# Half pages in tags of their own, no transferred lows, a sixth raw slot and other sets of seven-product pairs in a two-layer hybrid encoder

## The chip, the cores and the metric

The kernel runs on one core of one Trainium2 chip. The metric is the device time of one execution in microseconds. Before the change it is 2624.51 us, the median of three runs (2623.55 to 2626.14).

TensorE (PE in the profile) multiplies, VectorE (DVE) and ScalarE (ACT) prepare operands and combine results, GpSimd (POOL) issues one queue of transfers and does a few small powers, SyncE (SP) issues the other queue of transfers.

## The reference

Two layers of an encoder on 256 tokens of width 4096. Each layer reads its normalised input through one projection of 11264 columns, runs grouped attention on a half of the result and bidirectional retention on the other, and returns through a second projection of 4096 columns.

```python
for l in range(DEPTH):                       # DEPTH = 2, SEQ = 256, D_MODEL = 4096
    h = rmsnorm(x, norm_w[l])
    proj = h @ w_in[l]                       # 4096 x 11264
    aq, ak, av, ag, rq, rk, rv, rg = jnp.split(proj, SPLIT_POINTS, axis=-1)
    ...
    a_out = (jax.nn.silu(ag) * gqa_attention(aq, ak, av)).astype(x.dtype)
    ...
    r = bidirectional_retention(rq, rk, rv, log_gf, log_gb).transpose(0, 2, 1, 3)
    r = rmsnorm(r, ret_norm[l]).reshape(B, S, RET_WIDTH)
    r_out = (jax.nn.silu(rg.astype(jnp.float32)) * r).astype(x.dtype)
    x = x + jnp.concatenate([a_out, r_out], axis=-1) @ w_out[l]   # 4096 x 4096
return rmsnorm(x, final_norm)
```

All of it is float32. Nearly all the arithmetic is in the two projections of each layer.

## The kernel before

**Blocks and pairs.** A projection is cut into blocks of 1024 output columns: 11 blocks for the first projection of a layer (stages 0 and 2), 4 for the second (stages 1 and 3), 30 blocks in all. A block sums over 16 pairs of 128 rows (`p` 0 to 15). For one pair, the 256 tokens, the 256 rows and the 1024 columns make a 2 x 2 by 2 x 2 product of matrices. Eleven of the sixteen pairs compute it with eight products (`EIGHT_PRODUCTS`), five with seven (`SEVEN_PRODUCTS`, a Strassen-Winograd scheme). `SEVENS` has the five for each stage. The products gather in eight PSUM banks, `M1` to `M8`; `M1`, `M5`, `M6`, `M7` belong to the seven-product pairs alone and are lent to the attention and the retention between whiles.

**High and low parts.** A float32 operand is cut into a high part in the type fp32r and the rest, the low part. One product is then three matmuls: high weight by high token part, high weight by low token part (line 1461 of the kernel before), low weight by high token part (line 1471). The high part of the weights is a cast on ACT (`whi`), the low part a subtraction on DVE (`wlo`), both recorded on line 248.

**Pages.** A *page* is a weight tile of 128 x 2 x 512. Raw pages land in `wraw` (5 slots, 512 KB each, issued by SP on line 448). An eight-product pair has two pages, A and B, with four products each. A seven-product pair has four: A, the sum page T, B and the sum page U, with 2, 2, 1 and 2 products. The sums are DVE instructions (`wsum`), one of 1024 elements for T and two of 512 for U. Page B of a seven-product pair needs the second half alone, but takes a whole tile. High and low parts lie in a ring of five tiles each (`RING = 5`, tags `whi` and `wlo`): page n+5 may be begun only when page n has had its last product. `Weights.begin` begins the pages in that order.

**Transferred lows.** Some B pages (`FARS`) are *far*: a tile pair of their own (`fhi`, `flo`), where ACT casts the high part and writes its negative into `flo`, and a transfer by POOL (line 506) then adds the raw weights to it. Those pages cost DVE nothing. There are 44 of them.

**The start.** Pairs 0 and 1 of the first block are multiplied in plain float32, without a cut (`NATIVE`); their four pages wait in the tiles `fhi`, `flo` and two of `wsum`. The token operands of the other pairs are made as their chunks of two pairs land: ACT scales by the gain and casts (`x8h`, `x7h`), DVE makes the sums of a seven-product pair (`xf`) and the low parts (`x8l`, `x7l`).

**The order of the work** is fixed when the program is built. A planner walks through the matmuls, keeps its own times for PE, DVE and ACT, and puts the remaining work (`Lane` steps: combining, rotary, softmax, retention, normalisation) between the pages where `room` says that the next page's low part is still made in time. Its constants (`STEP_V`, `LANDING`, `STORE`, `EARLY`, `NEAR` and others) are costs and distances in microseconds or products. `LANDING`, `STORE` and `FETCH` are the times after which it takes a transfer as done.

Of the kernel before, what the change touches and what calls it, by code (L numbers as in the profile page):

```python
# [33 lines left out]
BLK = 32  # L34
ALL = slice(None)
PAGES = 13
RAWS = 5

RING = 5
FAR = 1  # L40

STEP_V = 1.6
STEP_S = 0.7

V_FIXED = 0.07
S_FIXED = 0.16

MM = {512: 0.2268, 256: 0.1177}
PASS = 0.1

LANDING = 11.0
STORE = 9.0
FETCH = 13.0
FAR_LANDING = 10.0
MARGIN = 0.5

RUSH = 1.5

EARLY = 0.7

ADD_AHEAD = 2.5

NEED = {"ak": 5, "ag": 3, "rk": 4, "rg": 4}

PE_REST = 1.8

TIGHT_A = 2
TIGHT_B = 3

AT_ONCE = 5  # L70

WARM = 20

SPLITS = 2

START = 1

SEVENS = ((3, 5, 7, 9, 11), (5, 7, 9, 10, 11), (3, 5, 7, 9, 11), (5, 7, 10, 11, 12))

EVER = sorted(set(_p for _s in SEVENS for _p in _s))  # L80
EIGHTS = [_p for _p in range(NP) if _p not in EVER]
# [4 lines left out]

WHOLE = 4

HOLD = 10

NEAR = 25

LATE = 20

FARS = ((2, 12), (1, 8), (12,), (15,))


AQ, AK, AV, AG, RQ, RK, RVO, RG = 0, 2048, 2560, 3072, 5120, 6144, 7168, 9216
# [105 lines left out]
EASY = ("M7",)  # L204


BANK_REST = 1.0
APART = 0.0

TOGETHER = 4  # L210

OTHER = True

TURNS = "01"

ABREAST = True
BANKS = ("M1", "M2", "M3", "M4", "M5", "M6", "M7", "M8")


# [43 lines left out]
def hybrid_encoder(  # L263
# [47 lines left out]
    def drop(n=1):  # L311

        held[0] -= n
        own(-n)
# [85 lines left out]
    class Weights:  # L400


        def __init__(self):
            self.pages = []
            for l in range(DEPTH):
                for w, n in ((w_in, N_IN), (w_out, N_OUT2)):
                    for b in range(n):
                        stage = 2 * l + (w is w_out)
                        for g in GROUPS[stage]:
                            start = (l, b) == (0, 0) and w is w_in  # L410
                            for slot in slots_of(g, stage, start):
# [24 lines left out]
            self.order = near[:RING]  # L436
            for g in self.pages:
                self.order += g.next
# [71 lines left out]

        def begin(self, g):

            g.begun = True
            if g.far:
                self.far_parts(g, self.taken())
            elif not g.seven:
                self.parts(g, self.taken(), then=self.load)
            elif g.kind == PAGE_A:
                self.sums_low(PAGE_T)
                self.a, self.b = self.taken(), self.taken()  # L520
                self.v = t(wp, [P, 2, NB], "wsum", 2)
                ve.tensor_sub(self.v, self.a, self.b[:, 0:1, :].to_broadcast([P, 2, NB]))
                self.parts(g, self.a)
            elif g.kind == PAGE_T:
                self.sums_low(PAGE_U)
                self.u = t(wp, [P, 2, NB], "wsum", 2)
                ve.tensor_add(self.u[:, 0, :], self.a[:, 1, :], self.v[:, 0, :])
                ve.tensor_sub(self.u[:, 1, :], self.u[:, 0, :], self.b[:, 1, :])
                self.load()
                self.parts(g, self.v)  # L530
            elif g.kind == PAGE_B:
                self.parts(g, self.b, (1,), self.load)
            else:
                self.parts(g, self.u)

        def sums_low(self, kind):

# [192 lines left out]
    class Turn:  # L730
# [18 lines left out]

        def step(self, forced=False):  # L750
            c = self.fetched
            if c < self.last and c < self.cut + 2 and (self.first or stored.get(c, 1e9) < now.t + (1e9 if forced else 0.0)) and held[0] + pledged() < PAGES - (2 if tasks else 0):
# [12 lines left out]
            return False  # L765
# [6 lines left out]
    using = []  # L772

    spare, taken, window, want, users, last_block = {}, {}, [0, False, 99], [0], set(), [False]

    def take_bank():

# [13 lines left out]

    def near(late=0):

        return window[1] and window[2] >= late or window[0] <= NEAR and not window[1]

    class Lane:
        def __init__(self, steps, heavy=True, need=0, own=0, owner=None, gate=None):
# [55 lines left out]
    def advance():  # L853

        clear()
        if not lanes + running():
            if waiting:
                split_step()
                return
            if turning and turning[0].step(True):  # L860
                return
        one = min(lanes + (running() or [tasks[0]]), key=lambda v: v.ready)
        now.wait(one.ready)
        one.step()
        clear()
# [464 lines left out]
    def block(after_pair, phase, then, first_order=False, order=LAST_ORDER, last=None, hurried=False):  # L1330
# [76 lines left out]
        def end_product(n, name, p, index, k, h):  # L1407
# [17 lines left out]
            if not g.uses and g in using:  # L1425
                using.remove(g)
                if g.whole:
                    for _ in range(1 if g is not weights.wholes[-1] else RING):
                        begun()
                for one in g.next:  # L1430
                    weights.begin(one)
# [401 lines left out]
```

## Time and profile before

| | |
|---|---|
| time, median of 3 runs | 2624.51 us |
| profiled execution: its own time, span of its instructions | 2624.09 us, 2622.3 us |
| DVE busy | 2231.7 us (85%), 2666 instructions |
| ACT busy | 1684.6 us (64%), 2411 instructions |
| POOL busy | 274.6 us (10%), 413 instructions |
| moved | 633.58 MB, 242 GB/s |
| granted clock of TensorE | 0.998 |

Matmuls overlap in this profile: one of 512 columns is listed with 389 ns, but the next starts 227 ns after it. A lost quarter of a microsecond can therefore hide in "busy". The weight loads (PEld) show it better: each matmul has one, of 188 ns, and in the steady state 39 ns of idle time stand ahead of it. Whatever the view of waits lists for PEld over that is time lost by TensorE.

### The profile page before, as it was taken

What the parts mean: (1) busy time and instruction counts of PE and PEld (TensorE: products, weight loads), DVE (VectorE), ACT (ScalarE), POOL (GpSimd) and SP (SyncE); (2) the same over time, 40 slices, a digit from 0 to 9 for tenths busy, and PEclk for the clock granted to TensorE, in tenths of its full rate; (3) what the DMA queues carried; (4) which work ended last, traced back from release to release, by engine and by line L of the source; (5) the groups of instructions that cost most, each with busy time, mean ns of one, the idle gap of its engine ahead of it and who ended that gap; (6) DMA issues with size and microseconds to landing.
All of it is one profiled execution on the core that took longest, in us unless ns stands there. A gap on an engine that the chain in (4) does not pass through costs nothing.

```text
span 2622.3 us, 33965 instructions
## 1 busy us (share of the span) xinstructions
PE 2604.2 (99%) x11650; PEld 2151.5 (82%) x11650; DVE 2231.7 (85%) x2666; ACT 1684.6 (64%) x2411; POOL 274.6 (10%) x413
## 2 busy tenths in 40 slices
PE   9999999999999999999999999999999999999998
PEld 7888888888888888888888888888888888878886
DVE  8798988898878889777998889898997798897768
ACT  7776667656555778556785666676565566775545
POOL 0010221120001000111101101211100010000000
PEclk9999999999999999999999999999999999999999
DMA  7888887877667766777767777778766666656775
GB/s 287 291 263 261 266 266 240 295 241 235 211 217 235 232 227 214 259 261 255 276 219 230 257 237 265 255 239 276 249 225 209 217 227 217 227 201 220 240 235 188
DMA packets 187151, 633.58 MB, mean 242 GB/s; under 512 B 22624, under 2 KB 29280, under 8 KB 186976
## 3 DMA queue, kind: packets, MB, share of 16 engines
q1 hardware_dynamic: 147760, 521.27, 56.6%
q0 software_dynamic: 39216, 110.12, 15.9%
q8 instruction: 91, 1.49, 0.2%
q14 instruction: 84, 0.69, 0.1%
HBM read 587.27 MB, written 44.04 MB: 241 GB/s over the span
## 4 chain that ended last, share of the span: by engine, by line
PE 94%; DVE 3%; issue 1%; ACT 1%; DMA 1%; SPq 0%; DVEq 0%; POOLq 0%; POOL 0%; ACTq 0%
PE M L1461 60%; PE M L1471 30%; DVE wlo L248 1%; PE M L945 1%; PE M L944 1%; PE M L943 1%; DMA wraw<-in_w_in 1%; DVE wsum L248 1%; PE M L1455 0%; ACT whi L248 0%; ACT ca L248 0%; DMA flo<-in_w_in 0%; DVE ca L248 0%; DVE x7l L248 0%; DVE ls L248 0%
## 5 line engine op out<-in xcount | busy, mean ns | idle before, releaser
L248 ACT CAST whi<-wraw 128x1024 fp32r<-128x1024 f32 (+1 forms) x912 | 878.5, 978 | 529.8 <-PE M L1461 346.2
L248 DVE TENSOR_TENSOR wlo<-wraw,whi 128x1024 fp32r<-128x1024 f32 (+1 forms) x912 | 1007.5, 1127 | 156.3 <-ACT whi L248 147.6
L1461 PE MATMUL M<-whi,x8h 128*128 128x512 f32 x2042 | 795.7, 390 | 0.2 <-DVE cb L248 0.2
L1461 PE MATMUL M<-whi,x8l 128*128 128x512 f32 x2042 | 795.2, 389 | 0.0
L1471 PE MATMUL M<-wlo,x8h 128*128 128x512 f32 x2042 | 586.3, 389 | 0.0
L1461 PE MATMUL M<-whi,x7h 128*128 128x512 f32 x1442 | 561.2, 389 | 1.0 <-ACT whi L248 1.0
L1461 PE MATMUL M<-whi,x7l 128*128 128x512 f32 x1442 | 561.0, 389 | 0.0
L248 ACT CAST whi<-wsum 128x1024 fp32r<-128x1024 f32 x300 | 315.9, 1053 | 212.4 <-PE M L1461 105.2
L1461 PEld LDWEIGHTS M<-whi,x8h 128*128 128x128 f32 x2042 | 383.4, 188 | 80.8 <-DVE cb L248 1.3
L1461 PEld LDWEIGHTS M<-whi,x8l 128*128 128x128 f32 x2042 | 383.4, 188 | 79.0 <-DVE x7l L248 0.2
L1471 PEld LDWEIGHTS M<-wlo,x8h 128*128 128x128 f32 x2042 | 382.1, 188 | 78.8
L1471 PE MATMUL M<-wlo,x7h 128*128 128x512 f32 x1442 | 442.1, 390 | 2.7 <-DVE wlo L248 2.4
L248 DVE TENSOR_TENSOR wlo<-wsum,whi 128x1024 fp32r<-128x1024 f32 x300 | 365.9, 1220 | 42.6 <-ACT whi L248 42.4
L1471 PEld LDWEIGHTS M<-wlo,x7h 128*128 128x128 f32 x1442 | 269.5, 188 | 63.3 <-DVE wlo L248 8.2
L1461 PEld LDWEIGHTS M<-whi,x7h 128*128 128x128 f32 x1442 | 270.7, 188 | 57.8 <-ACT whi L248 1.4
L1461 PEld LDWEIGHTS M<-whi,x7l 128*128 128x128 f32 x1442 | 270.7, 188 | 56.3
L248 DVE TENSOR_TENSOR wsum<-wraw 128x1024 f32<-128x1024 f32 x150 | 182.5, 1216 | 29.9 <-DMA wraw<-in_w_out 14.0
L506 POOL DMA_DIRECT2D flo<-in_w_in x32 | 29.2, 912 | 819.5 <-ACT flo L248 814.4
L248 DVE TENSOR_TENSOR wsum<-wsum,wraw 128x512 f32<-128x512 f32 x150 | 103.8, 692 | 5.2
L248 DVE TENSOR_TENSOR wsum<-wraw,wsum 128x512 f32<-128x512 f32 x150 | 102.4, 683 | 0.1
L248 DVE TENSOR_TENSOR cb<-cb,M 128x512 f32<-128x512 f32 x90 | 60.8, 679 | 23.8 <-PE M L1471 23.8
L248 ACT ACTIVATE pr<-M,st,rs 128x256 f32<-128x256 f32 x64 | 35.5, 559 | 48.5 <-DVE st L248 48.5
(232 smaller groups left out, 1961.3 us busy)
## 6 DMA issues: line engine op xcount, KB each, us to landing
wraw<-in_w_in SPq DMA_DIRECT2D x700, 512.0 KB, 4.5
wraw<-in_w_out SPq DMA_DIRECT2D x256, 512.0 KB, 4.4
flo<-in_w_in POOLq DMA_DIRECT2D x32, 512.0 KB, 7.4
full<-next_dram POOLq DMA_DIRECT2D x18, 512.0 KB, 8.4
kv<-kv_dram POOLq DMA_DIRECT2D x16, 512.0 KB, 7.4
p_dram<-room POOLq DMA_DIRECT2D x64, 128.0 KB, 2.9
pT<-p_dram POOLq DMA_DIRECT2D x16, 512.0 KB, 9.3
flo<-in_w_out POOLq DMA_DIRECT2D x11, 512.0 KB, 7.6
```

The source lines that it names most:

```text
L248: return call(out, *args, **kwargs)
L506: nc.gpsimd.dma_start(g.lo[h], g.src[0][:, h, :], accum_op=ALU.add)
L943: nc.tensor.matmul(out, a[0], b[0], start=start, stop=False)
L944: nc.tensor.matmul(out, a[0], b[1], start=False, stop=False)
L945: nc.tensor.matmul(out, a[1], b[0], start=False, stop=stop)
L1461: nc.tensor.matmul(acc[name], a[i], g.hi[h], start=m == first[name] and not i, stop=False)
L1471: nc.tensor.matmul(acc[name], a, g.lo[h], start=False, stop=m == final[name])
```

## The change

The weights' bookkeeping changes in one point of form and the planner gets other constants.

- Page B of a seven-product pair becomes a half page, 128 x 512, in tags `bhi` and `blo` with two buffers each (`HALVES = 2`). It leaves the ring of five. It is begun when its page T has been begun (its raw page is then known) and one of the two buffers is free.
- `FARS` is empty: the 44 far pages become ordinary pages of the ring, with their low parts made by DVE. The tags `fhi` and `flo` are gone.
- `RAWS` is 6.
- The four plain pages of the start lie in the pool of working pages (`pg`), not in `fhi`, `flo` and `wsum`.
- `SEVENS` names other pairs, still five for each stage. Pairs 3 and 4, and 10 and 11, now follow each other directly in stages 0 and 2; 10, 11 and 12 in stages 1 and 3.
- Constants of the planner. `LANDING` falls from 11 to 9.5, `STORE` from 9 to 5, `PE_REST` from 1.8 to 1.2, `EARLY` grows from 0.7 to 1.3, `V_FIXED` from 0.07 to 0.1, `STEP_S` from 0.7 to 1.5, `PASS` from 0.1 to 0.3, `TIGHT_B` from 3 to 9. `START`, the pages begun ahead of the first block, is 2 for 1. `ABREAST` and `OTHER` are off: the last two output tiles of a layer's second projection are worked one after the other.
- `force` lets the planner open the window for lent banks when nothing else is ready.

```diff
-RAWS = 5
+RAWS = 6
...
+HALVES = 2
...
-STEP_V = 1.6
-STEP_S = 0.7
+STEP_V = 1.2
+STEP_S = 1.5
...
-PASS = 0.1
-
-LANDING = 11.0
-STORE = 9.0
+PASS = 0.3
+
+LANDING = 9.5
+STORE = 5.0
 FETCH = 13.0
...
-SEVENS = ((3, 5, 7, 9, 11), (5, 7, 9, 10, 11), (3, 5, 7, 9, 11), (5, 7, 10, 11, 12))
+SEVENS = ((3, 4, 6, 10, 11), (4, 6, 10, 11, 12), (3, 4, 6, 10, 11), (4, 6, 10, 11, 12))
...
-FARS = ((2, 12), (1, 8), (12,), (15,))
+FARS = ((), (), (), ())
...
-                                one.kept = None
+                                one.kept, one.half = None, one.seven and one.kind == PAGE_B
+                                one.allowed = one.wanted = False
...
-            near = [g for g in self.pages if not g.far and not g.whole]
+            near = [g for g in self.pages if not g.far and not g.whole and not g.half]
+            half = [g for g in self.pages if g.half]
+            for g, then in zip(half, half[HALVES:]):
+                g.next.append(then)
+            for g in half[:HALVES]:
+                g.allowed = True
+            for i, g in enumerate(self.pages):
+                g.third = next(v for v in self.pages[i:] if v.half) if g.seven and g.kind == PAGE_T else None
...
-            tag, bufs, dt = (("fhi", FAR, F32R), ("flo", FAR, F32R), ("wsum", 2, F32), ("wsum", 2, F32))[n]
-            g.raw = f32(t(wp, [P, 2, NB], tag, bufs, dt))
+            g.raw = page([P, 2, NB], "whole")
...
-            hi = t(wp, [P, 2, NB], "whi", RING, F32R)
-            lo = t(wp, [P, 2, NB], "wlo", RING, F32R)
-            halves = self.places(g, hi, lo, halves)
+            if g.half:
+                g.hi, g.lo = ({1: t(wp, [P, NB], v, HALVES, F32R)} for v in ("bhi", "blo"))
+            else:
+                hi = t(wp, [P, 2, NB], "whi", RING, F32R)
+                lo = t(wp, [P, 2, NB], "wlo", RING, F32R)
+                halves = self.places(g, hi, lo, halves)
...
+            if g.half:
+                g.allowed = True
+                if g.wanted:
+                    self.begin_half(g)
+                return
             g.begun = True
...
-            elif g.kind == PAGE_B:
-                self.parts(g, self.b, (1,), self.load)
+                g.third.wanted, g.third.raw = True, self.b
+                if g.third.allowed:
+                    self.begin_half(g.third)
             else:
                 self.parts(g, self.u)
+
+        def begin_half(self, g):
+
+            g.begun = True
+            self.parts(g, g.raw, (1,), self.load)
...
-OTHER = True
+OTHER = False
...
-ABREAST = True
+ABREAST = False
```

TensorE has the same matmuls in both programs, 11,635 of them; they read other tiles and stand in another order. DVE gets 43 more low parts of 1024 elements and one of 512 (instructions `wlo`), plus the low parts of the 150 half pages under the new name `blo`. ACT loses the 44 negated copies, POOL the 44 adding transfers.

The order on DVE in the first block of the last stage, pairs 10 to 12, before (`wsum` is a sum page, the last number of a row its elements, the numbers behind the names tell the tiles apart):

```order
L248 TENSOR_TENSOR wlo_20368<-wsum_20353,whi_20367 128x1024
L248 TENSOR_TENSOR wlo_20384<-wraw_20279,whi_20383 128x512
L248 TENSOR_TENSOR wlo_20396<-wsum_20362,whi_20395 128x1024
L248 TENSOR_TENSOR wsum_20423<-wraw_20292,wraw_20338 128x1024
L248 TENSOR_TENSOR wlo_20426<-wraw_20292,whi_20425 128x1024
L248 TENSOR_TENSOR x8l_20410<-ca_19594,x8h_20409 128x256 x2
L248 TENSOR_TENSOR wsum_20437<-wraw_20292,wsum_20423 128x512
L248 TENSOR_TENSOR wsum_20437<-wsum_20437,wraw_20338 128x512
L248 TENSOR_TENSOR wlo_20443<-wsum_20423,whi_20442 128x1024
```

and the same place after:

```order
L250 TENSOR_TENSOR wlo_20330<-wsum_20313,whi_20329 128x1024
L250 TENSOR_TENSOR blo_20333<-wraw_20215,bhi_20332 128x512
L250 TENSOR_TENSOR wlo_20353<-wsum_20324,whi_20352 128x1024
L250 TENSOR_TENSOR wsum_20368<-wraw_20222,wraw_20284 128x1024
L250 TENSOR_TENSOR wlo_20371<-wraw_20222,whi_20370 128x1024
L250 TENSOR_TENSOR wsum_20386<-wraw_20222,wsum_20368 128x512
L250 TENSOR_TENSOR wsum_20386<-wsum_20386,wraw_20284 128x512
L250 TENSOR_TENSOR wlo_20392<-wsum_20368,whi_20391 128x1024
```

TensorE takes pairs 10, 11 and 12 in the same order in both. The DVE rows are the same up to the name of the half page and the place of the token operand `x8l`. The ring differs: `wlo_20443` (page T of pair 11) lies where `wlo_20356`, page A of pair 10, lay. `wlo_20392` lies where the page ahead of pair 10's page A lay, since the half page no longer counts.

The order on DVE in the first block of the program, from the end of pair 4's token operand to pair 4's page A, after (`xf` and `x7l` are token operands of seven-product pairs, `x8l` of eight-product pairs):

```order
L250 TENSOR_TENSOR x7l<-xf,x7h 128x640
L250 TENSOR_TENSOR x8l<-full,x8h 128x512
L250 TENSOR_TENSOR wsum<-wraw 128x1024
L250 TENSOR_TENSOR xf<-xf,full 128x128
L250 SCALAR_TENSOR_TENSOR xf<-xf,full 128x128
L250 TENSOR_TENSOR xf<-full 128x128
L250 TENSOR_TENSOR xf<-full,xf 128x128
L250 TENSOR_TENSOR x8l<-full,x8h 128x512
L250 TENSOR_TENSOR x7l<-full,x7h 128x256
L250 TENSOR_TENSOR wlo<-wraw,whi 128x1024
```

Before, pair 4 had eight products and its two pages stood between those of pair 3, so that the next seven-product page came two pairs later. Now the operands of pairs 4 and 5 and the greater part of those of pairs 6 and 7 stand ahead of pair 4's first low part.

And on ACT in the same place, after:

```order
L250 CAST x7h<-xf 128x640
L250 CAST x8h<-full 128x512
L250 ACTIVATE full<-full,nw 128x256 x4
L250 ACTIVATE xf<-full 128x128
L250 CAST x7h<-full 128x256
L250 CAST x8h<-full 128x512
L250 CAST whi<-wraw 128x1024
L250 CAST x7h<-xf 128x640
L250 ACTIVATE full<-full,nw 128x256 x2
L250 CAST whi<-wraw 128x1024
```

The first `whi` here is page A of pair 4, the second page A of pair 5. The casts of chunk 3 (pairs 6 and 7) have come ahead of it.

More of the change, by code (lines that the diff above doesn't have):

```diff
@@ L36 @@
 PAGES = 13
-RAWS = 5
+RAWS = 6
 RING = 5
 FAR = 1
-STEP_V = 1.6
-STEP_S = 0.7
-V_FIXED = 0.07
+HALVES = 2
+STEP_V = 1.2
+STEP_S = 1.5
+V_FIXED = 0.1
 S_FIXED = 0.16
 MM = {512: 0.2268, 256: 0.1177}
-PASS = 0.1
-LANDING = 11.0
-STORE = 9.0
+PASS = 0.3
+LANDING = 9.5
+STORE = 5.0
 FETCH = 13.0
-FAR_LANDING = 10.0
+FAR_LANDING = 9.0
 MARGIN = 0.5
[L57 to L65, printed above, removed]
+RUSH = 2.5
+EARLY = 1.3
+ADD_AHEAD = 3.0
+NEED = {"ak": 4, "ag": 3, "rk": 5, "rg": 4}
+PE_REST = 1.2
 TIGHT_A = 2
-TIGHT_B = 3
-AT_ONCE = 5
+TIGHT_B = 9
+AT_ONCE = 3
 WARM = 20
 SPLITS = 2
-START = 1
-SEVENS = ((3, 5, 7, 9, 11), (5, 7, 9, 10, 11), (3, 5, 7, 9, 11), (5, 7, 10, 11, 12))
+START = 2
+SEVENS = ((3, 4, 6, 10, 11), (4, 6, 10, 11, 12), (3, 4, 6, 10, 11), (4, 6, 10, 11, 12))
 EVER = sorted(set(_p for _s in SEVENS for _p in _s))
@@ L87 @@
 WHOLE = 4
-HOLD = 10
-NEAR = 25
-LATE = 20
-FARS = ((2, 12), (1, 8), (12,), (15,))
+HOLD = 4
+NEAR = 40
+LATE = 10
+FARS = ((), (), (), ())
 AQ, AK, AV, AG, RQ, RK, RVO, RG = 0, 2048, 2560, 3072, 5120, 6144, 7168, 9216
@@ L204 @@
 EASY = ("M7",)
-BANK_REST = 1.0
+BANK_REST = 0.8
 APART = 0.0
 TOGETHER = 4
-OTHER = True
+OTHER = False
 TURNS = "01"
-ABREAST = True
+ABREAST = False
 BANKS = ("M1", "M2", "M3", "M4", "M5", "M6", "M7", "M8")
@@ L437, in __init__ @@
             for g in self.pages:
-                self.order += g.next
+                self.order += [v for v in g.next if not v.half]
             self.todo = [src for g in self.order for src in g.src]
@@ L751, in step @@
             c = self.fetched
-            if c < self.last and c < self.cut + 2 and (self.first or stored.get(c, 1e9) < now.t + (1e9 if forced else 0.0)) and held[0] + pledged() < PAGES - (2 if tasks else 0):
+            if c < self.last and c < self.cut + 2 and (self.first or c in stored and stored[c] < now.t + (1e9 if forced else 0.0)) and held[0] + pledged() < PAGES - (2 if tasks else 0):
                 self.fetch(c)
@@ L774, in hybrid_encoder @@
     spare, taken, window, want, users, last_block = {}, {}, [0, False, 99], [0], set(), [False]
+    force = [False]
     def take_bank():
@@ L792, in near @@
     def near(late=0):
-        return window[1] and window[2] >= late or window[0] <= NEAR and not window[1]
+        return force[0] or window[1] and window[2] >= late or window[0] <= NEAR and not window[1]
     class Lane:
@@ L861, in advance @@
                 return
-        one = min(lanes + (running() or [tasks[0]]), key=lambda v: v.ready)
+            force[0] = True
+        ready = lanes + running()
+        force[0] = False
+        if not ready:
+            now.wait(now.t + 0.5)
+            return
+        one = min(ready, key=lambda v: v.ready)
         now.wait(one.ready)
@@ L1427, in end_product @@
                 if g.whole:
+                    drop()
                     for _ in range(1 if g is not weights.wholes[-1] else RING):
```

## The prediction

> **What bounds the kernel now.** I read the page first, for the engine that is never free.
>
> ```profile
> span 2622.3 us, 33965 instructions
> PE 2604.2 (99%) x11650; PEld 2151.5 (82%) x11650; DVE 2231.7 (85%) x2666; ACT 1684.6 (64%) x2411; POOL 274.6 (10%) x413
> PE 94%; DVE 3%; issue 1%; ACT 1%; DMA 1%; SPq 0%; DVEq 0%; POOLq 0%; POOL 0%; ACTq 0%
> 206.74 1.81 PE M L1461 x8
> ```
>
> TensorE is busy 99% of the span and carries 94% of the chain that ended last. Eight matmuls take 1.81 us there, so one takes 0.227 us. Since the change keeps every matmul, all that it can gain is what TensorE loses between them. For that I read the waits of the weight loads.
>
> ```profile
> PEld M L1471 <- DVE wlo L248: 8.2, 15, 1.7
> PEld M L1461 <- ACT whi L248: 1.4, 1, 1.4
> PEld M L1461 <- DVE cb L248: 1.3, 4, 0.6
> PEld M L1461 <- DVE ca L248: 0.5, 1, 0.5
> L1471 PEld LDWEIGHTS M<-wlo,x8h 128*128 128x128 f32 x2042 | 382.1, 188 | 78.8
> ```
>
> The last row gives the ordinary gap, 78.8 us over 2042 loads, 0.039 us each. Taking it off 16 waits leaves 9.6 - 0.6 = **9.0 us** lost to page parts that came late, of which 1.4 us is one high part. Another 1.6 us went to banks that were still being read (`cb`, `ca`). The stretches show where:
>
> ```profile
> 545.00:633.00 88.00, 87.03 (x388) 71.60 (x387) 79.78 (x93) 54.16 (x64) 11.65 (x18) 1.00 0.76 255
> 1777.00:1865.00 88.00, 88.00 (x400) 73.15 (x400) 77.50 (x93) 53.98 (x75) 11.37 (x21) 1.00 0.79 258
> 2305.00:2393.00 88.00, 86.42 (x379) 70.67 (x378) 71.04 (x80) 54.58 (x74) 2.71 (x3) 1.00 0.66 217
> 2600.00:2622.30 22.30, 10.03 (x45) 7.97 (x43) 11.56 (x24) 6.80 (x14) 1.12 (x2) 0.82 0.51 189
> ```
>
> The columns after the stretch are its length, then PE, PEld, DVE, ACT and POOL. Most stretches are like the second, with TensorE never idle. The first and third hold single events. The last has the tail, 22.30 - 10.03 = 12.3 us after the last matmul, which the change leaves as it was: the rows of DVE, ACT and SP from the last combination on are the same.
>
> **The gain: a longer lead.** The largest loss is in the third stretch.
>
> ```profile
> 2326.66 1.33 ACT L248 CAST x8h<-ca 128x256 fp32r<-128x256 f32 x4
> 2327.88 1.06 ACT L248 CAST whi<-wraw 128x1024 fp32r<-128x1024 f32 x1
> 2332.11 1.22 DVE L248 TENSOR_TENSOR wlo<-wsum,whi 128x1024 fp32r<-128x1024 f32 x1
> 2333.39 0.73 PE L1471 MATMUL M<-wlo,x7h 128*128 128x512 f32 x2 [1.27 <-DVE wlo L248]
> ```
>
> ACT cast token operands first, the high part of pair 11's page A came at 2328.9, and DVE then ran page A, two sums and page T without a pause; page T ended at 2333.3 and TensorE had waited 1.27 us. How early a page can be begun is set by the ring. Page T of pair 11 lies where page A of pair 10 lay, so between the last use of the one and the first need of the other's low part TensorE has pair 10's T, B and U (2+1+2 products), pair 11's A (2) and two thirds of T: 7 x 3 x 0.227 + 4 x 0.227 = 5.7 us. In the change the B page no longer takes a tile; the slot is free one page earlier, by page A's 2 x 3 x 0.227 = 1.36 us, or by 2.04 us where the half page of the pair before lies between too. The waits on low parts average 8.2 / 15 = 0.55 us and the longest is 1.7 us, so this extra lead covers fourteen and at worst leaves 0.3 us of the last. The single high part waited for a raw page,
>
> ```profile
> ACT whi L248 <- DMA wraw<-in_w_in: 109.8, 52, 5.2
> ```
>
> and a sixth raw slot lets SP ask for each page some 2.7 us of products sooner (an eight-product page, 12 x 0.227), more than the 1.4 us lost. I take **8.0 of the 9.0 us** as gained; the bounds are 9.0 (all) and 4.5 (half, if work is put where the new lead is, and uses it up). The 1.6 us at the banks stays.
>
> **What the lows cost.** The transferred lows return to DVE.
>
> ```profile
> L248 DVE TENSOR_TENSOR wlo<-wraw,whi 128x1024 fp32r<-128x1024 f32 x755 | 906.2, 1220 | 147.7 <-ACT whi L248 144.9
> L248 ACT ACTIVATE flo<-fhi 128x1024 fp32r<-128x1024 f32 (+1 forms) x44 | 46.3, 1053 | 1.4
> flo<-in_w_in POOLq DMA_DIRECT2D x32, 512.0 KB, 7.4
> ```
>
> 44 x 1.22 = 53.7 us more DVE work takes its share from 85% to 87%. ACT gets 46.3 us back, and 44 transfers of 0.5 MB go, 23 of 633 MB. Spread over 30 blocks it is 1.8 us of DVE work per block; the fullest stretch quoted has DVE free for 88.0 - 79.8 = 8.2 us. So I cost the lows at 0: the idle time of DVE inside each block hides them. Without that cover they cost up to 1.22 us each.
>
> **What the start costs.** Pairs 3 and 4 are now both seven-product pairs with nothing between, while the token operands are still being made. Rows of before give the step from one start to the next:
>
> ```profile
> 17.75 1.23 DVE L248 TENSOR_TENSOR wsum<-wraw 128x1024 f32<-128x1024 f32 x1 [0.21 <-DMA wraw<-in_w_in]
> 20.02 0.82 DVE L248 TENSOR_TENSOR x7l<-xf,x7h 128x640 fp32r<-128x640 f32 x1
> 20.76 1.22 DVE L248 TENSOR_TENSOR wlo<-wraw,whi 128x1024 fp32r<-128x1024 f32 x1
> 21.89 0.69 DVE L248 TENSOR_TENSOR wsum<-wraw,wsum 128x512 f32<-128x512 f32 x1
> 23.23 1.22 DVE L248 TENSOR_TENSOR wlo<-wsum,whi 128x1024 fp32r<-128x1024 f32 x1
> 24.36 0.68 DVE L248 TENSOR_TENSOR x8l<-full,x8h 128x512 fp32r<-128x512 f32 x1
> 24.96 0.28 DVE L248 TENSOR_TENSOR xf<-xf,full 128x128 f32<-128x128 f32 x1
> 25.90 1.22 DVE L248 TENSOR_TENSOR wlo<-wraw,whi 128x1024 fp32r<-128x1024 f32 x1
> 27.03 0.42 DVE L248 TENSOR_TENSOR x7l<-full,x7h 128x256 fp32r<-128x256 f32 x1
> 27.37 0.68 DVE L248 TENSOR_TENSOR x8l<-full,x8h 128x512 fp32r<-128x512 f32 x1
> 26.32 0.39 PE L1461 MATMUL M<-whi,x7h 128*128 128x512 f32 x1
> ```
>
> So 1.13 us for 1024 elements, 0.74 for 640, 0.60 for 512, 0.34 for 256, 1.34 for the two sums, 0.94 for the four `xf`. The wait at 17.75 is for pair 3's raw pages, the third and fourth issued in both programs; that start stays. From there to the low part of pair 4's page A DVE has six of 1024 (6.78), the sums (1.34), three of 512 (1.80), three of 256 (1.02), two of 640 (1.48) and three sets of `xf` (2.82): 15.24 us, so it ends at 33.0. TensorE starts pair 3 at 26.32, needs 7 x 3 x 0.227 = 4.8 us, then 0.9 us for the high products of pair 4's page A, and wants the low part at 32.0: **1.0 us late**. Pair 5's first page follows 1.8 us of high products later; ahead of its low part DVE has 640, the sums and 1024 again, 3.2 us against TensorE's 0.45 + 1.8: another 0.9 us. ACT has the casts of three chunks ahead of these two high parts, and DVE must wait for some of them, which I put at 0.5 us. Together **2.4 us**, between 1.0 (page A alone) and 4.5 (the next two pages as late as these).
>
> **The sum.** 2622.3 - 8.0 + 2.4 = 2616.7 us of span. The profiled run's own time is 2624.09, 1.8 above its span, which gives 2618.5; the median of the runs shown, 2624.51, lies 0.4 above that run, which gives **2618.9 us**.
>
> **Rivals.**
>
> *The lead is used up.* The planner fills DVE and ACT to what its own times allow, and its allowances moved with the ring. If half the waits remain (4.5 us gained) and the start costs 2.4 to 4.5 us, the time is 2622.4 to 2624.5, no change. For it: the waits sit where token operands are made between pages, and that work stays. Against it: at the place quoted the rows of DVE are the same, and only the slot comes earlier.
>
> *Late transfers, slower.* `LANDING`, `STORE` decide when a step is put on ACT or DVE; both queues are in order, so a step whose transfer has not landed holds every page part behind it.
>
> ```profile
> q<-q_dram POOLq DMA_DIRECT2D x8, 512.0 KB, 11.1
> q_dram<-cb POOLq DMA_DIRECT2D x32, 128.0 KB, 4.4
> ca<-x_dram POOLq DMA_DIRECT2D x3, 512.0 KB, 11.1
> cb<-x_dram POOLq DMA_DIRECT2D x3, 512.0 KB, 14.3
> L905 POOL DMA_DIRECT2D q_dram<-cb x32 | 17.9, 572 | 53.8 <-DVE cb L248 53.7
> ```
>
> A query tile takes four issues of 0.57, 4.4 to land and 11.1 for the fetch, 17.8 us, where the planner allowed 9 + 13 = 22 and now allows 18. A residual tile needs 11.1 or 14.3 where it allowed 11 and now allows 9.5. Lateness decides once it is over the lead of 5.7 + 1.4 = 7.1 us less a page's making (1.06 + 1.22), some 4.8 us. If eight query tiles and seven residual tiles each lose 1 us over it, 15 us return: 2633.9. Against it: 23 MB fewer transfers on that queue, and a gate in most steps that opens later than the allowance. [...]
>
> *The lows come out.* If DVE's idle time lies in the wrong places and a third of the 44 lows lands ahead of a page that TensorE waits for, 15 x 1.22 = 18 us return, 2637. Against it: the fullest stretch is 91% busy.
>
> *The start alone is worse.* With 4.5 us there and 8.0 gained, 2621.0, no change.
>
> **How the numbers follow.** What a measurement here can tell is about 0.2%, 5.2 us: faster is under 2619.3, slower over 2629.8. The forecast has a chance of 0.50, with 2615.8 (9.0 gained, the start at 1.0: 2616.5, less some of the bank waits) to 2622 for its own range, of which four fifths lie under 2619.3 as far as the terms go: 0.40 faster, 0.10 the same. The lead used up 0.17, of which 0.02 faster, the start alone 0.15, of which 0.05 is faster since the gain may be the full 9.0, late transfers 0.12 and lows coming out 0.06, of which 0.14 together slower. That is 0.47 faster, 0.39 the same, 0.14 slower. The range is 2614.5 to 2628: about 0.05 is left out below it and 0.15 above, the dearer half of each slower case among that.
>
> **What would show it.** Right: PEld's waits on `wlo` under 2 us in total outside the first 60 us, TensorE idle in no stretch of the last stage, no wait of ACT for a raw page that reaches TensorE, and in the first block 1 to 4 us of waits around 31 to 37 us, at the first pages of pairs 4 and 5. Half right: the start's waits there, with others left at the joints of stages. Wrong: waits of ACT or DVE for `q`, `pT`, `ca` or `cb` followed by waits of TensorE, or DVE over 95% in a block with TensorE idle beside it.

## The result, and the profile after

The change runs in 2618.67 us, the median of 14 runs (2618.06 to 2619.76). The kernel before ran beside it on the same chip in 2624.73 us (14 runs, 2623.07 to 2626.14). The ratio is 0.9978, with a 95% interval of 0.9969 to 0.9986. The forecast was 2618.9 us, in a range of 2614.5 to 2628.

The page of the profile after, first part and the chain of waits:

```profile
span 2617.1 us, 33631 instructions
PE 2601.1 (99%) x11650; PEld 2152.7 (82%) x11650; DVE 2279.7 (87%) x2711; ACT 1627.2 (62%) x2366; POOL 238.4 (9%) x368
PE 98%; DVE 1%; DMA 0%; issue 0%; ACT 0%; SPq 0%; POOLq 0%; POOL 0%; DVEq 0%; ACTq 0%
```

The span is 5.2 us shorter and TensorE carries 98% of the chain in place of 94%. VectorE is at the forecast 87%. The waits of the weight loads after, outside the first 60 us:

```profile
PEld M L1492 <- issue: 0.4, 2, 0.2
PEld M L1502 <- DVE wlo L250: 0.3, 1, 0.3
```

and from 22 to 60 us, where the kernel before had none:

```profile
PEld M L1492 <- ACT whi L250: 2.0, 2, 1.4
PEld M L1502 <- DVE wlo L250: 1.4, 2, 0.8
```

The columns are total, times and longest, in us. Before, page parts and banks held the weight loads for 11.4 us after the start. Now it is 0.7 us, and 3.4 us came up at the start. A weight load's wait counts more than TensorE loses, since a product may still be running, so it is not time lost by TensorE as it stands, as the section on the profile before has it. The better sum is over the starts of successive matmuls: whatever lies above the ordinary 0.22675 us (512 columns) or 0.1195 us (256 columns). From 22 us on this sum is 10.65 us before and 5.30 us after. Of the 5.30, 2.81 lie between 32.6 and 38.5 us. So the rest of the run gained 8.15 us and the start lost 2.81: 5.34 us together, against 5.2 us of span.

The stretches that the prediction showed, after (length, PE, PEld, DVE, ACT, POOL):

```profile
545.00:633.00 88.00, 88.00 (x393) 72.87 (x392) 81.92 (x97) 49.04 (x56) 11.21 (x18) 1.00 0.75 255
2305.00:2393.00 88.00, 88.00 (x390) 72.87 (x389) 73.99 (x78) 51.20 (x64) 1.79 (x2) 1.00 0.70 231
2600.00:2617.10 17.10, 5.04 (x23) 3.84 (x21) 6.84 (x16) 5.35 (x10) 1.12 (x2) 0.72 0.66 246
```

TensorE is never idle in the two that held single events, with VectorE busier in both. The tail is 17.10 - 5.04 = 12.1 us; it was 12.3.

### The profile page after: what moved, and what is told of

It reads as the page before. It is cut to its first block, busy times and chain, and to the rows that moved or that the text cites. A ratio compares the mean times of both kernels' runs of the same rounds, so it can differ in the third digit from the quotient of the medians.

```text
span 2617.1 us, 33631 instructions
## 1 busy us (share of the span) xinstructions
PE 2601.1 (99%) x11650; PEld 2152.7 (82%) x11650; DVE 2279.7 (87%) x2711; ACT 1627.2 (62%) x2366; POOL 238.4 (9%) x368
## 4 chain that ended last, share of the span: by engine, by line
PE 98%; DVE 1%; DMA 0%; issue 0%; ACT 0%; SPq 0%; POOLq 0%; POOL 0%; DVEq 0%; ACTq 0%
PE M L1492 63%; PE M L1502 32%; PE M L974 1%; PE M L975 1%; PE M L973 1%; DMA wraw<-in_w_in 0%; DVE wlo L250 0%; DVE wsum L250 0%; DVE x7l L250 0%; DVE xf L250 0%; DVE cb L250 0%; DVE x8l L250 0%; SPq L466 0%; ACT full L250 0%; SPq L1715 0%
## 5 line engine op out<-in xcount | busy, mean ns | idle before, releaser
L250 ACT CAST whi<-wraw 128x1024 fp32r<-128x1024 f32 x806 | 834.0, 1047 | 567.0 <-PE M L1492 503.2
L250 DVE TENSOR_TENSOR wlo<-wraw,whi 128x1024 fp32r<-128x1024 f32 x806 | 962.7, 1213 | 128.9 <-ACT whi L250 127.2
L1492 PE MATMUL M<-whi,x8h 128*128 128x512 f32 x2368 | 922.2, 389 | 0.1
L1492 PE MATMUL M<-whi,x8l 128*128 128x512 f32 x2368 | 921.7, 389 | 0.0
L1502 PE MATMUL M<-wlo,x8h 128*128 128x512 f32 x2368 | 679.1, 389 | 0.2 <-DVE wlo L250 0.2
L1492 PEld LDWEIGHTS M<-whi,x8h 128*128 128x128 f32 x2368 | 444.6, 188 | 92.7 <-ACT whi L250 0.6
L1492 PEld LDWEIGHTS M<-whi,x8l 128*128 128x128 f32 x2368 | 444.6, 188 | 92.0 <-DVE xf L250 0.2
L1502 PEld LDWEIGHTS M<-wlo,x8h 128*128 128x128 f32 x2368 | 442.7, 188 | 91.3 <-DVE wlo L250 0.7
L1492 PE MATMUL M<-whi,x7h 128*128 128x512 f32 x1140 | 443.8, 389 | 1.0 <-ACT whi L250 1.0
L1492 PE MATMUL M<-whi,x7l 128*128 128x512 f32 x1140 | 443.5, 389 | 0.0
L1502 PE MATMUL M<-wlo,x7h 128*128 128x512 f32 x1140 | 341.8, 389 | 0.3 <-DVE wlo L250 0.3
L1492 PEld LDWEIGHTS M<-whi,x7h 128*128 128x128 f32 x1140 | 214.0, 188 | 46.3 <-ACT whi L250 1.4
L1502 PEld LDWEIGHTS M<-wlo,x7h 128*128 128x128 f32 x1140 | 213.7, 188 | 45.3 <-DVE wlo L250 1.1
L1492 PEld LDWEIGHTS M<-whi,x7l 128*128 128x128 f32 x1140 | 214.0, 188 | 44.3
L250 DVE TENSOR_TENSOR blo<-wraw,bhi 128x512 fp32r<-128x512 f32 x150 | 102.5, 684 | 0.0
L250 ACT CAST bhi<-wraw 128x512 fp32r<-128x512 f32 x150 | 92.2, 615 | 0.0
```

The source lines that it names most:

```text
L250: return call(out, *args, **kwargs)
L1492: nc.tensor.matmul(acc[name], a[i], g.hi[h], start=m == first[name] and not i, stop=False)
L1502: nc.tensor.matmul(acc[name], a, g.lo[h], start=False, stop=m == final[name])
```

## The experiments

All ran beside the kernel before, whose medians were 2624.56, 2624.43 and 2624.56 us in the three groups of four. A planner orders the work, so a kernel with another ring or another constant also gets another order. That turned out to matter most. Line numbers shift a little where an edit adds or drops one: the products are L1491 and L1501 in some kernels, L1492 and L1502 in others.

### 1 to 3: the parts of the layout

**The half pages back in the ring of five.** Everything else of the change stays.

```diff
-one.kept, one.half = None, one.seven and one.kind == PAGE_B
+one.kept, one.half = None, False
...
+elif g.kind == PAGE_B:
+    self.parts(g, self.b, (1,), self.load)
```

> The changed kernel with page B of a seven-product pair put back into the ring of five (whole tiles); no transferred lows, six raw slots, the new sets and the planner's constants stay. Theory of the lead (the gain came because the half page left the ring): the lead falls by 1.4 to 2.0 us, the weight loads wait 4 to 10 us in total for low parts again, outside the first 60 us, and the time is 2622 to 2629. Rival (the sets, the constants or the raw slot brought the gain): within 1.5 us of the changed kernel, 2617 to 2620.5, with waits on low parts under 2 us.

Measured: 2663.15 us, 1.0146 of before (1.0132 to 1.0160). The direction was right and the size was far off. The weight loads' waits:

```profile
PEld M L1501 <- DVE wlo L250: 13.5, 15, 1.6
PEld M L1491 <- DVE ca L250: 13.0, 2, 6.5
PEld M L1491 <- issue: 8.6, 6, 3.4
PEld M L1491 <- ACT whi L250: 6.5, 5, 2.6
```

The first row is what the lead theory speaks of. The second is something else: two waits of 6.5 us for a bank. TensorE's timeline at the first of them, and the stretch behind it (the column after POOL is the granted clock):

```profile
911.51 0.39 PE L1491 MATMUL M<-whi,x7l 128*128 128x512 f32 x1
917.96 0.79 PE L1491 MATMUL M<-whi,x7h 128*128 128x512 f32 x1 [6.05 <-DVE ca L250]
918.55 0.63 PE L1491 MATMUL M<-whi,x7l 128*128 128x512 f32 x1
```

```profile
918.00:922.40 4.40, 4.40 (x11) 3.43 (x12) 3.48 (x5) 2.53 (x3) 0.00 (x0) 0.50 0.61 215
```

A retention head has written its twelve products into a bank that the seven-product pairs share. ScalarE sums their squares, GpSimd takes a power, and VectorE's `ca<-M,rst,ca` reads the bank and frees it. TensorE waits 6.05 us for that, and runs eleven matmuls behind it at half the clock. Counted between starts, this place costs 8.6 us and its twin in the second layer 8.2. Two more such places (738 and 2054 us) cost 5.1 and 3.5. These four make 25.4 of the 48.0 us that TensorE loses in this kernel.

**A ring of six whole tiles**, which takes the memory of the half pages' own tags:

```diff
-RING = 5
+RING = 6
```

> As the run before, but with a ring of six whole tiles in each tag, which takes the same memory as the half pages' two tags. Theory of the lead: one more tile gives back 1.4 us or more of products in every place, so the waits on low parts fall to under 3 us and the time is within 2 us of the changed kernel, 2617 to 2621. Rival (what counts is that the half page has an order of its own, begun as soon as its sum page is begun): as slow as the run before, 2622 or more.

Measured: 2633.15 us, 1.0032 (1.0020 to 1.0043). One more slot brings 30 us back, and the waits on low parts fall from 13.5 to 4.7 us. But two stalls of the other kind stand at 999 and 2303 us:

```profile
999.23 0.77 PE L1491 MATMUL M<-whi,x7h 128*128 128x512 f32 x1 [4.33 <-DVE ca L250]
```

```profile
999.20:1004.50 5.30, 5.28 (x13) 4.14 (x14) 5.30 (x8) 3.99 (x9) 0.00 (x0) 0.50 0.29 99
```

They cost 7.1 and 7.4 us, again with a half clock behind them. The time lies outside what was expected of the lead (2617 to 2621 us). Without the two stalls the sum between starts would be 19.7 - 14.5 = 5.2 us, that of the change.

**Five raw slots** in the change, in place of six:

```diff
-RAWS = 6
+RAWS = 5
```

> The changed kernel with five raw slots for six. Theory of the lead: only waits on high parts whose raw page is late can return, 1.4 us of them before; 2618.5 to 2620.5. Rival (the sixth slot carries much of the gain): 2622 or more, with waits of ACT for raw pages that TensorE shares.

Measured: 2622.51 us, 0.9992 (0.9983 to 1.0001). The sixth slot is worth 3.8 us, not the 1.4 us of one high part: four groups of waits come up, two in each layer, for high and low parts, and ScalarE waits for raw pages of the first projection again. That these waits of ScalarE make the four groups is likely, but was not followed from row to row. Here with five slots, then with six:

```profile
ACT whi L250 <- DMA wraw<-in_w_in: 104.9, 75, 5.3
```

```profile
ACT whi L250 <- DMA wraw<-in_w_in: 24.8, 13, 5.7
```

### 4 and 8: the start

The change also begins two pages ahead of the first token operands, where one was begun before. The fourth kernel takes that back in the change, the eighth puts it into the kernel before:

```diff
-START = 2
+START = 1
```

> The changed kernel with one page begun ahead of the first block for two (START 1), so that DVE and ACT make pair 3's token operand and both pages of pair 2 before pair 3's sum pages; nothing else moves after the first 60 us. Theory of the start (the waits of 2.8 us at 32 to 38 us come from the order of DVE and ACT there): by the rows' durations the low part of pair 4's page A is 0.7 us early instead of 1.0 us late, the waits fall under 0.8 us, and the time is 2615.3 to 2617. Rival (pairs 3 and 4 side by side ask for more work than there is time, in any order): within 0.6 us of the changed kernel, 2618 to 2619.3.

> The kernel before with one constant changed: two pages begun at the start in place of one. If the waits at the start come from the second begun page alone, they appear here too: 2626.5 to 2628 us. If they need pairs 3 and 4 side by side, there is no difference: within 1 us of 2624.6.

Measured: the change with one page begun takes 2616.55 us, 0.9968 (0.9956 to 0.9981), and is the fastest kernel of the study. The kernel before with two takes 2629.62 us, 1.0020 (1.0011 to 1.0029). The waits of the weight loads from 22 to 60 us fall from 3.4 us to the first row below in the one, and rise from nothing to the second in the other:

```profile
PEld M L1502 <- DVE wlo L250: 0.8, 2, 0.5
```

```profile
PEld M L1471 <- DVE wlo L248: 3.5, 5, 1.2
```

So the second begun page makes waits at the start, with pairs 3 and 4 side by side (the change) and without (the kernel before, where they come later, at 39 to 52 us). The eighth kernel is slower than the 2626.5 to 2628 us expected: counted between starts, 3.3 us of its loss lie before 60 us and another 1.1 us behind. One begun page is no safeguard either: the twelfth kernel below, with one, loses 2.2 us before 60 us under the change's other constants. ScalarE's timeline in the change shows how the second page does it. The second page's cast waits 1.51 us for its raw page, and a token chunk stands behind it on ScalarE's queue; the last two rows are page A of pair 4, and TensorE's wait for it:

```profile
14.18 1.04 ACT L250 CAST whi<-wraw 128x1024 fp32r<-128x1024 f32 x1 [1.51 <-DMA wraw<-in_w_in]
15.13 1.70 ACT L250 ACTIVATE full<-full,nw 128x256 f32<-128x256 f32 x4
31.47 1.04 ACT L250 CAST whi<-wraw 128x1024 fp32r<-128x1024 f32 x1
32.56 0.50 PE L1492 MATMUL M<-whi,x7h 128*128 128x512 f32 x1 [0.98 <-ACT whi L250]
```

With one page begun, the chunk comes first:

```profile
12.31 1.70 ACT L250 ACTIVATE full<-full,nw 128x256 f32<-128x256 f32 x4
14.93 1.04 ACT L250 CAST whi<-wraw 128x1024 fp32r<-128x1024 f32 x1
28.07 1.04 ACT L250 CAST whi<-wraw 128x1024 fp32r<-128x1024 f32 x1
```

It starts 2.8 us earlier, and page A of pair 4 is cast 3.4 us earlier, well ahead of TensorE.

### 5 and 12: the layout and the planner's constants, one without the other

The fifth kernel is the change with the planner's other constants of before, the twelfth the kernel before with those of the change (`START` stays as each had it, and the planner's code, with `force`, stays with its layout). Nine of these constants differ between the two programs without being named in the list of the change: `FAR_LANDING`, `RUSH`, `ADD_AHEAD`, `NEED`, `AT_ONCE`, `HOLD`, `NEAR`, `LATE` and `BANK_REST`. Part of the fifth kernel's edit:

```diff
-STEP_V = 1.2
-STEP_S = 1.5
...
+STEP_V = 1.6
+STEP_S = 0.7
...
-LANDING = 9.5
-STORE = 5.0
...
+LANDING = 11.0
+STORE = 9.0
...
-BANK_REST = 0.8
+BANK_REST = 1.0
...
```

> The changed layout of memory (half pages in tags of their own, six raw slots, no transferred lows, the new sets, two pages begun at the start) with all the planner's constants of before: transfers allowed 11 and 9 us where the change allows 9.5 and 5, among others. If the longer lead is what the change is worth, most of the gain stays: 2617 to 2621 us, with waits on low parts under 3 us outside the start. If the late-transfer rival is right, the longer allowances make it faster than the change: under 2616 us. If the new constants carry the gain, the waits come back: 2623 us or more.

> The kernel before (ring of five with the half pages, five raw slots, transferred lows, its own sets and one page begun) with all the other planner's constants of the change. If the constants carry the gain, 2622 us or less. If they only fit the new layout, as the old ones only fit the old (the change with the old ones took 2653 us), it is slower than before: 2628 us or more, with stalls at the joints of stages.

Measured: 2653.45 us, 1.0108 (1.0094 to 1.0121), and 2643.21 us, 1.0070 (1.0057 to 1.0082). Neither half gains alone:

| | constants of before | constants of the change |
|---|---|---|
| layout of before | 2624.7 | 2643.2 |
| layout of the change | 2653.5 | 2618.7 |

The new layout with the old constants has few waits on low parts (outside the first 60 us), but stalls at banks of the heads, put down to `issue` in the weight loads' waits and to `ca` in TensorE's timeline. They cost 20.4 us between starts, and two stalls at token operands (`x7l`) another 11.2:

```profile
PEld M L1492 <- issue: 15.8, 3, 7.7
PEld M L1502 <- DVE wlo L250: 2.7, 5, 0.8
```

```profile
1004.57 0.77 PE L1492 MATMUL M<-whi,x7h 128*128 128x512 f32 x1 [7.52 <-DVE ca L250]
```

The old layout with the new constants has the opposite, thirty-one waits on low parts, and not the stalls at the joints of stages that were expected (its one stall at a bank, at 652 us, costs 4.9 us):

```profile
PEld M L1471 <- DVE wlo L248: 18.6, 31, 2.0
```

### 6 and 7: the lows and the sets

The ring of five as in the first experiment, with the 44 low parts transferred again; and the change with the sets of before and five raw slots:

```diff
-FARS = ((), (), (), ())
+FARS = ((2, 12), (1, 8), (12,), (15,))
```

```diff
-RAWS = 6
+RAWS = 5
-SEVENS = ((3, 4, 6, 10, 11), (4, 6, 10, 11, 12), (3, 4, 6, 10, 11), (4, 6, 10, 11, 12))
+SEVENS = ((3, 5, 7, 9, 11), (5, 7, 9, 10, 11), (3, 5, 7, 9, 11), (5, 7, 10, 11, 12))
```

> The ring of five that also holds the half pages, as in the first experiment (2663 us), with the 44 low parts transferred as before the change. If the first experiment lost 44 us since VectorE's 54 us of lows have no cover when the lead is short, most of that comes back: 2622 to 2632 us. If the short lead and the order that follows from it lost it whatever the lows do, the time stays at 2650 us or more.

> The change with the sets of five pairs of before and, since these need more memory, five raw slots: to be compared with the change with five raw slots, 2622.5 us. By the prediction the waits at 31 to 37 us come from pairs 3 and 4 side by side, so without them 2 to 3 us of waits go there: 2619 to 2621 us if nothing else moves. If two begun pages alone make these waits, they stay, and the time is 2622 us or more.

Measured: 2639.05 us, 1.0056 (1.0043 to 1.0068), and 2652.74 us, 1.0109 (1.0095 to 1.0123). The sixth kernel lies between its two cases. Transferring the lows gives back 24.1 of the 38.6 us that the first experiment lost. It is not shown that the 53.7 us of VectorE's work that they save do this: the weight loads' waits on low parts only fall from 13.5 to 10.3 us. What falls most is TensorE's wait for banks that `ca` still reads, which is a matter of the order. The first experiment, then this kernel:

```profile
PE M L1491 <- DVE ca L250: 19.1, 6, 6.1
```

```profile
PE M L1491 <- DVE ca L250: 3.5, 3, 1.5
```

The seventh kernel is inconclusive on the sets. It is 30 us above the change with five raw slots, nearly all of it in single stalls of up to 8.8 us between 1004 and 1042 and between 2314 and 2366 us, the three largest of them at token operands (`x7l` twice, `x8h` once). At the start, from 22 to 70 us, the low parts still cost waits:

```profile
PEld M L1502 <- DVE wlo L250: 4.3, 7, 0.9
```

So pairs 3 and 4 side by side are not needed for waits at the start, as the eighth kernel shows too. They bear on the place: between 32.6 and 38.5 us the loss is 0.8 us here and 2.8 in the change, and the rest comes later.

### 9 to 11: what the stalls at the banks hang on

In the first experiment GpSimd's power took 5.61 us at 911 us, with VectorE at work beside it:

```profile
911.38 5.61 POOL L396 TENSOR_TENSOR rst<-rst,half 128x2 f32<-128x2 f32 x1 [48.19 <-DVE rst L250]
911.80 1.22 DVE L250 TENSOR_TENSOR wlo<-wsum,whi 128x1024 fp32r<-128x1024 f32 x1
912.94 1.22 DVE L250 TENSOR_TENSOR wsum<-wraw 128x1024 f32<-128x1024 f32 x1
914.07 2.35 DVE L250 TENSOR_TENSOR wlo<-wraw,whi 128x1024 fp32r<-128x1024 f32 x2
917.03 0.87 DVE L250 SCALAR_TENSOR_TENSOR ca<-M,rst,ca 128x256 f32<-128x256 f32 x2 [0.60 <-POOL rst L396]
```

I took the long power for the cause of the stall. The ninth kernel makes VectorE wait for each power, so that nothing of VectorE's runs beside it:

```diff
 rsqrt(st, st, MT, RV)
+nc.vector.tensor_scalar_mul(st, st, 1.0)
```

> The first experiment (ring of five holds the half pages, 2663.15 us) with one small VectorE instruction more behind each of the 16 powers that GpSimd computes for the retention heads: it reads the power's result, so VectorE waits for the power at once and runs nothing beside it; the order of everything else is the same. In the first experiment two of these powers took 5.6 us where most take 0.7, with five VectorE instructions running back to back beside them, and TensorE stood 6 us behind each. If VectorE's work held the power up, the two powers take about 0.7 us, TensorE's two stalls shrink from 6.2 to about 1.3 us, the half-rate matmuls behind them go too, and the time falls by 10 to 14 us: 2649 to 2653. If GpSimd is slow there for a reason of its own, the powers stay long and the time stays at 2660 us or more.

Measured: 2667.64 us, 1.0164 (1.0150 to 1.0178). The same place:

```profile
912.85 0.71 POOL L396 TENSOR_TENSOR rst<-rst,half 128x2 f32<-128x2 f32 x1 [48.22 <-DVE rst L250]
913.59 0.17 DVE L1244 TENSOR_SCALAR rst<-rst 128x2 f32<-128x2 f32 x1 [0.83 <-POOL rst L396]
914.33 1.22 DVE L250 TENSOR_TENSOR wlo<-wsum,whi 128x1024 fp32r<-128x1024 f32 x1
918.88 0.86 DVE L250 SCALAR_TENSOR_TENSOR ca<-M,rst,ca 128x256 f32<-128x256 f32 x2
919.80 0.79 PE L1491 MATMUL M<-whi,x7h 128*128 128x512 f32 x1 [6.36 <-DVE ca L250]
```

All sixteen powers now take about 0.7 us, so VectorE's work had held the two long ones up. But the theory of the stall falls: TensorE still waits 6.36 us. The power is ready at 913.6, and the read of the bank comes at 918.88, because the order has put a table, a low part, a sum and two more low parts between. The queue of VectorE sets the stall, not the power.

The tenth kernel changes one constant of the first experiment back to that of before, the eleventh lowers one of the second:

```diff
-BANK_REST = 0.8
+BANK_REST = 1.0
```

```diff
-LANDING = 9.5
+LANDING = 9.0
```

> The first experiment with one planner constant changed back to that of before, the time a bank is allowed to rest: 1.0 for 0.8 us. By it the products that stood right in front of a bank still being read at 738 us (and at 2054 us in the second layer) get others between. If what the first experiment lost there came from that order and not from the lead, the 5.1 and 3.5 us of these two places go: 2653 to 2656 us, with the low-part waits as they were. If the short lead makes these stalls in one way or another, they come up elsewhere: 2660 us or more.

> The ring of six whole tiles (second experiment, 2633.15 us) with one planner constant changed, the transfers' allowance 9.0 for 9.5 us, by which the last twelve products of the joints at 999 and 2303 us no longer stand right in front of their own bank. If a longer lead is the gain and only these two joints kept the ring of six from it, 14.5 us of loss go: 2617 to 2621 us, as the change. If half pages in tags of their own carry more than the lead, it stays at 2624 us or more.

Measured: 2658.93 us, 1.0132 (1.0117 to 1.0148), and 2645.00 us, 1.0076 (1.0064 to 1.0089). The tenth loses the stalls at 738 and 2054 us as expected, and gains 4 us, less than the 8.6 us of the two places: four new places with waits on high and low parts cost 1.1 to 1.2 us each. The eleventh missed. The stalls at 999 and 2303 us are gone, two as long stand at 908 and 2217 us, and the waits on low parts are back at 11.5 us with a ring of six:

```profile
PEld M L1501 <- DVE wlo L250: 11.5, 14, 1.7
PEld M L1491 <- DVE ca L250: 10.2, 2, 5.1
```

A change of half a microsecond in one allowance moved the time by 12 us.

## Why the prediction was right

**What bounds the kernel.** Right: every matmul stayed (11,650 rows in both profiles), and the whole difference lies in gaps between them.

**The gain, 8.0 us.** Measured 8.15, and at the places named: no weight load waits on a high part after 60 us, one on a low part, for 0.3 us. That the total came so close is in part luck, since sizes inside the term were off and made up for each other. Counted between starts, page parts had cost 7.4 us, not 9.0, and 7.2 of them went; the banks, which were to stay, had cost 1.0 us, and that went too. And the sixth raw slot carries about half of the 8.15 us, not 1.4: with five slots the change gains 4.2 us after the start, and by its time it can't be told from the kernel before (2.1 us faster, with an interval that takes in no change).

**A longer lead as the reason.** Supported, not shown, since it was always tried together with another order. The seven kernels with the half pages in a ring of five wait 8.2 (before) to 18.6 us on low parts. Of the seven with a slot more, five wait 0.8 to 4.7 us, the start included (the change 1.7), but the seventh experiment waits 7.4 and the eleventh 11.5. So the rival "the lead is used up" is real for some constants and sets, and not for the change's. A kernel with another lead and the very same order was not tried.

**What the step left out.** The prediction carried the order of before over to the change and asked only which waits go. The order is written anew for every layout and every constant, and in six kernels (the first, second, fifth and ninth to eleventh) it put 14 to 29 us of stalls at banks of retention heads that are written again too soon. In the fifth and the seventh, 11 and 22 us of stalls stand at token operands that came late. In the change there is none of either. At a head near the end of the first stage TensorE has 3 us of other products to run until the bank is free:

```profile
993.01 0.28 PE L975 MATMUL M<-vh,wTl 128*128 128x256 f32 x1
995.43 1.07 PE L1502 MATMUL M<-wlo,x7h 128*128 128x512 f32 x4
995.47 0.88 DVE L250 SCALAR_TENSOR_TENSOR ca<-M,rst,ca 128x256 f32<-128x256 f32 x2 [0.88 <-POOL rst L396]
```

The forecast needed that and did not price it. It came out since the loss that it counted was there, and this order has nothing in its place. As far as the working goes that is luck: of the twelve other kernels ten were slower than the kernel before.

**The lows at nothing.** Right in the change: VectorE works 48.0 us more, and no more than 0.3 us of waits on a low part is left after the start. What the lows cost without cover stays open: with the short lead the kernel with the same lows on VectorE is 24 us slower, but most of that is stalls at banks.

**The start, 2.4 us.** Measured 2.81, at 32.6 to 38.5 us, in the place and size forecast. That the size fits is luck: the working had the wrong emphasis and the wrong cause. Counted between starts, the high parts of pairs 4 and 5 cost 1.7 us, where ScalarE was put at 0.5, and the low parts that were to cost 1.0 and 0.9 cost 0.6 and 0.5. And it takes the second begun page: with one, pairs 3 and 4 still side by side, the loss there is 0.4 us. The second page's cast waits for a raw page at the head of ScalarE's queue. That is the mechanism of the late transfers, in another place than where the prediction looked for it. How much of the 2.4 us lost between one page and two is that wait, and how much the other order behind it, was not separated.

**The rivals.** Late transfers of query and residual tiles: no weight load in the change waits behind one, and longer allowances, set back together with the other constants, made it slower, not faster. Lows coming out, and the start alone at 4.5 us: not seen.

## What to carry to other kernels

Where a planner writes the order, a change of layout and the planner's constants are one change: each half alone can lose several times what both gain, so neither is to be judged on its own. When the bound engine is 99% busy, add up the gaps between the starts of its instructions by place, since a wait of its loads overstates the loss and a mean hides single stalls. Look for a small instruction that frees a shared buffer and is queued behind large ones; in the ninth kernel, shortening what it waits for helped nothing while the queue stood.

## What was not expected of the hardware

**A stall of TensorE costs about half as much again.** After each idle time of 4 us or more, the next 8 to 13 matmuls of 512 columns came 0.427 us apart in place of 0.227, at a granted clock of 0.50, for 4 to 6 us. A stall of 4.3 us cost 7.1 us and one of 6.05 us 8.6. Single gaps between starts of 1.65 us in the kernel before and 2.2 us in the ninth were followed by the ordinary pace; of two of 3.48 us in the first experiment, one was followed by eight slow matmuls and its twin in the other layer by none. The Trainium skill, page TensorE: Matmul & The Clock Gate, section What's actually happening, gives a free-running window of some 3.4 us, after one of which idle the clock is halved; by that, a gap between one and two windows may or may not hold a whole one. For single gaps the rows agree.

Two short gaps close together did it too. In the first experiment, idle times of 1.20 and 0.59 us were followed by eight matmuls at the slow pace:

```profile
2340.53 0.50 PE L1491 MATMUL M<-whi,x7h 128*128 128x512 f32 x1 [1.20 <-ACT whi L250]
2342.32 0.97 PE L1501 MATMUL M<-wlo,x7h 128*128 128x512 f32 x2 [0.59 <-DVE wlo L250]
2343.09 0.63 PE L1491 MATMUL M<-whi,x8h 128*128 128x512 f32 x1
2343.51 0.63 PE L1491 MATMUL M<-whi,x8l 128*128 128x512 f32 x1
```

The same two gaps in the ninth kernel, at 2347.6 and 2349.4 us, were followed by the ordinary pace. So no length of a single gap decides it here.

**VectorE holds a GpSimd instruction up.** The power of 128x2 elements takes 0.71 us with VectorE idle, 1.52 us where one instruction of 1.22 us had started 0.26 us ahead of it, and 5.61 us where VectorE works back to back until 916.4 us, ending 0.6 us after that. It is not held up where VectorE starts later (at 990.35 us in the kernel before, an `x8l` starts 0.18 us after the power, which takes 0.71), nor where one of VectorE's two operands lies in a bank (at 698.42 us there, `D<-M,D` runs beside 0.5 us of a power of 0.71). The middle case, in the change:

```profile
988.01 1.22 DVE L250 TENSOR_TENSOR wlo<-wraw,whi 128x1024 fp32r<-128x1024 f32 x1
988.27 1.52 POOL L396 TENSOR_TENSOR rst<-rst,half 128x2 f32<-128x2 f32 x1 [81.25 <-DVE rst L250]
```

The ninth kernel brought the long ones to 0.71 us. The Trainium skill, page SBUF — State Buffer, section SBUF: two separate sides, says that VectorE instructions with two operands in SBUF and GpSimd instructions that read SBUF lock each other out of a shared port pair; these durations agree with it. No run tried it on larger GpSimd work.
